# Spreading the RMS-norm factors of an encoder trunk: four fp32 matmuls on a diagonal, or two wide ones on its rounded parts

## The chip, the cores and the metric

One core of a Trainium2 chip runs the whole kernel in one launch. The metric is device microseconds of an execution, least is best. "Before" has three timed runs and one profiled execution.

## The reference

One layer on 2048 tokens of width 1024. Two sub-layers each begin with an RMS norm, scaled and shifted by a conditioning vector:

```python
def rmsnorm(x, g):
    y = x * lax.rsqrt(jnp.mean(x * x, axis=-1, keepdims=True) + EPS)
    return y * g
...
mod = silu(c) @ w_ada + b_ada
sh1, sc1, gt1, sh2, sc2, gt2 = split(mod, 6)
h = rmsnorm(x, g_norm1) * (1.0 + sc1) + sh1
proj = h @ w_in                                  # q, k, v of two groups of 8 heads
o_sb = stick_breaking_attention(...)             # strictly causal
o_ca = chunked_relpos_attention(...)             # own chunk of 64 and 8 before, learned bias
x = x + gt1 * (concat(o_sb, o_ca) @ w_o)
h = rmsnorm(x, g_norm2) * (1.0 + sc2) + sh2
x = x + gt2 * (square(relu(h @ w1)) @ w2)
```

All data is float32. What the change touches is the row of factors rsqrt(mean(x*x) + EPS), one factor for each token.

## The kernel before

Activations lie transposed: features on the 128 partitions, tokens along the free axis, in four blocks of 512 tokens (tb 0 to 3). A tile of 128x512 is one of eight feature slices of a block. Nearly every large product is done three times on rounded parts: an operand is split into a high part, rounded to the type that TensorE takes at one matmul a product (F32R in the code), and a low part, the rest; high x high, high x low and low x high add up in PSUM.

There are three stages. The first projects: block 3 comes first, with its weights, then the blocks 2, 1 and 0 are normed while the projections of the block before go on. The attention stage runs units of one head and one block of queries; between its steps it places further projections and parts of the output projection. The MLP runs its two products as seven products of half-size blocks each (classes First and Second), with the norms of blocks 1 and 0 put between the first steps of a Second phase.

A norm has these steps. ScalarE squares the eight slices and VectorE adds them up (norm_sums; norm2 for the MLP). TensorE sums over the partitions with four matmuls that use the sums as the stationary operand and a column of ones (norm_columns): this leaves the tokens on the partitions, 128 x 4 numbers. VectorE scales them and GpSimd takes the power and one refining step (norm_powers, rsqrt). To bring the factors back to one row that every partition holds, VectorE multiplies the identity with them (norm_diagonal: four diagonal blocks of 128x128 side by side), and TensorE multiplies a 128x128 matrix of ones with the diagonals (norm_spread: four fp32 matmuls of 128 columns). VectorE then multiplies x by the result in PSUM (first stage, tile names pra) or copies it into a row tile (MLP, psr).

Seven norms are spread this way. The first one, block 3 of the first stage, has its own code and calls norm_spread itself. Three go through start_norm (L464) for the blocks 2, 1 and 0 of the first stage. Two in the attention stage (tile prm) are written out in finish_row. Two go through norm2 (L1329) in the MLP. start_norm and norm2 call norm_rstd (L194) in a job called second, and the spread in a job called third some steps later; the jobs stand in lists that count steps.

The order of work is the program's: TensorE is kept in the order of the code, so are ScalarE, VectorE and GpSimd in the first stage, and nearly every DMA is issued on SyncE's queue.

Memory is given out in pools, those of the left side upward and those marked right downward. Left in the first stage stand, in this order: cpool (constants), rp, ring, hxp, np_ (the norms' tiles, L252), padn (a tile of 128 bytes that nothing uses, L253), stp (staging, tag st of six buffers of 128x2x512, L255) and wp (nine weight parts, L256). The staging ring takes every tile that is stored to DRAM. In the MLP, right: accp (tag c, twelve buffers of 128x512, function kept), hop 0 and 1 (split activations h) and np2; hop 2 and 3 are on the left.

In the attention stage each finished pair of heads is split into a tile os, of which there is one buffer, and stored to scr_m (function keep, L734).

Of the kernel before, what the change touches and what calls it, by code (L numbers as in the profile page):

```python
# [9 lines left out]
F32 = mybir.dt.float32  # L10
F32R = mybir.dt.float32r
BF16 = mybir.dt.bfloat16
AF = mybir.ActivationFunctionType
ALU = mybir.AluOpType
# [4 lines left out]
P = 128  # L19
# [6 lines left out]
TB = 512  # L26
# [53 lines left out]
def encoder_kernel(ctx, tc, xT, c, g1, g2, w_in, w_rest, gqk, bias, w_o, w1, w2, w_ada, b_ada, out):  # L80
    nc = tc.nc
    act, dve, pool, sp = nc.scalar, nc.vector, nc.gpsimd, nc.sync
    pe = Ordered(tc, nc.tensor)
# [3 lines left out]
    cpool = ctx.enter_context(tc.tile_pool(name="cpool", bufs=1))  # L87
# [27 lines left out]
    ident = cpool.tile([P, P], F32, name="ident")  # L115
    make_identity(nc, ident)
    ones = cpool.tile([P, P], F32, name="ones")
    pool.memset(ones, 1.0)
    zero = cpool.tile([P, 1], F32, name="zero")
    pool.memset(zero, 0.0)  # L120
    mhalf = cpool.tile([P, 2 * NH], F32, name="mhalf")
# [29 lines left out]
    def norm_sums(pl, src, tg, eng=None, square=None):  # L151

        acc = pl.tile([P, TB], F32, tag="nsa", name=f"nsa{tg}")
        for k in range(KT):
            x = src(k)
            if k == 0:
                act.activation(acc, x, AF.Square)
                continue
            sq = square(k) if square else pl.tile([P, TB], F32, tag="nsq", name=f"nsq{tg}_{k}")
            if square and k == KT - 1:  # L160
                pool.tensor_tensor(sq, x, x, op=ALU.mult)
                sq, last = last, sq
            else:
                act.activation(sq, x, AF.Square)
            if square and k == KT - 2:
                last = sq
                continue
            (eng or dve).tensor_tensor(acc, acc, last if square and k == KT - 1 else sq, op=ALU.add)
        if square:
            dve.tensor_tensor(acc, acc, sq, op=ALU.add)  # L170
        return acc

    def norm_columns(pp, acc, tg):
        pv = pp.tile([P, TB], F32, tag="ps", name=f"pv{tg}")
        for i in range(4):
            pe.matmul(pv[:, i : i + 1], acc[:, i * P : (i + 1) * P], ones[:, 0:1], start=True, stop=True)
        return pv

    def norm_powers(pl, pv, tg):
        v = pl.tile([P, 4], F32, tag="nv", name=f"nv{tg}")  # L180
        dve.tensor_scalar(v, pv[:, 0:4], 1.0 / D, EPS, op0=ALU.mult, op1=ALU.add)
        y = pl.tile([P, 4], F32, tag="ny", name=f"ny{tg}")
        t = pl.tile([P, 4], F32, tag="nt", name=f"nt{tg}")
        rsqrt(y, v, t)
        return y

    def norm_diagonal(pl, y, tg):
        dg = pl.tile([P, 4, P], F32, tag="ndg", name=f"ndg{tg}", bufs=1)
        dve.tensor_tensor(
            dg, ident.unsqueeze(1).to_broadcast([P, 4, P]), y.unsqueeze(2).to_broadcast([P, 4, P]), op=ALU.mult  # L190
        )
        return dg

    def norm_rstd(pl, pp, acc, tg, meanwhile=None):  # L194
        y = norm_powers(pl, norm_columns(pp, acc, tg), tg)
        if meanwhile:
            meanwhile()
        return norm_diagonal(pl, y, tg)

    def norm_spread(pp, dg, tg):  # L200
        pr = pp.tile([P, TB], F32, tag="ps", name=f"pr{tg}")
        for i in range(4):
            pe.matmul(pr[:, i * P : (i + 1) * P], ones, dg[:, i, :], start=True, stop=True)
        return pr
# [42 lines left out]
    pa, er = ctx.enter_context(ExitStack()), ctx.enter_context(ExitStack())  # L247
    if True:
# [1 line left out]
        adaw = er.enter_context(tc.tile_pool(name="adaw", bufs=4, side="right"))  # L250
        hp = er.enter_context(tc.tile_pool(name="hp", bufs=1, side="right"))
        np_ = pa.enter_context(tc.tile_pool(name="np_", bufs=2))  # L252
        padn = pa.enter_context(tc.tile_pool(name="padn", bufs=1))  # L253
        padn.tile([P, 32], F32, tag="pad", name="padn")
        stp = pa.enter_context(tc.tile_pool(name="stp", bufs=6))  # L255
        wp = pa.enter_context(tc.tile_pool(name="wp", bufs=WT))  # L256
        ppc = er.enter_context(tc.tile_pool(name="ppC", bufs=1, space=PSUM))
        pp, pq = Banks(zb), Banks(db)
# [80 lines left out]
        def stage(nm):  # L339
            return stp.tile([P, 2, TB], F32R, tag="st", name=f"st{nm}")  # L340
# [123 lines left out]
        def start_norm(tb, wait, more):  # L464
            tg = f"a{tb}"
            acc = norm_sums(np_, lambda k: xts[tb][k], tg)

            def second():
                dg = norm_rstd(np_, pq, acc, tg)

                def third():
                    r = norm_spread(pq, dg, tg)
                    for k, x in enumerate(xts[tb]):
                        dve.scalar_tensor_tensor(x, x, aff[:, 0, k : k + 1], r, op0=ALU.mult, op1=ALU.mult)

                norms.add(more, third)

            norms.add(wait, second)
# [18 lines left out]
        act, dve, pool = (Ordered(tc, e) for e in (act, dve, pool))  # L497
# [20 lines left out]
        for k in range(2):  # L518
            load_first(k)
        acc = norm_sums(  # L520
            np_, lambda k: xts[3][k], "a3",
            square=lambda k: stp.tile([P, TB], F32, tag="qh", name=f"nsqa3_{k}", bufs=6),
        )
# [15 lines left out]
        dg = np_.tile([P, 4, P], F32, tag="ndg", name="ndga3", bufs=1)  # L539
# [139 lines left out]
    if True:  # L679
# [536 lines left out]
        op = ph.enter_context(tc.tile_pool(name="op", bufs=2))  # L1216
# [14 lines left out]
        for i in range(len(steps) + LAG):  # L1231
# [29 lines left out]
            if i + 1 < len(steps):  # L1261
                u, st = steps[i + 1]
# [23 lines left out]
    if True:  # L1286
# [3 lines left out]
        accp = pm.enter_context(tc.tile_pool(name="accp", bufs=12, side="right"))  # L1290
        hop = {k: pm.enter_context(tc.tile_pool(name=f"hop{k}", bufs=1, side="right")) for k in range(2)}
        np2 = pm.enter_context(tc.tile_pool(name="np2", bufs=2, side="right"))
        pp = Banks(zb, zb, ab, db, zb, zb, ab, db)
# [18 lines left out]
        def temp(nm):  # L1312
            return tp.tile([P, TB], F32, tag="t", name=f"t{nm}")
# [4 lines left out]
        def bank(nm):  # L1318
            return pp.tile([P, TB], F32, tag="ps", name=f"ps{nm}")
# [3 lines left out]
        def at(n, job):  # L1323
            jobs.setdefault(n, []).append(job)
# [4 lines left out]
        def norm2(tb, step):  # L1329

            acc = rp.tile([P, TB], F32, tag="r", name=f"r{tb}")
            xs = {}

            def load(k):
                xs[k] = temp(f"xn{tb}_{k}")
                sp.dma_start(xs[k], scr_x[tb, k])

            def add(k):
                x = xs.pop(k)
                act.activation(x if k else acc, x, AF.Square)  # L1340
                if k:
                    dve.tensor_tensor(acc, acc, x, op=ALU.add)

            def second():
                dg = norm_rstd(np2, pp, acc, f"m{tb}")

                def third():
                    pr = bank(f"r{tb}")
                    for i in range(4):
                        pe.matmul(pr[:, i * P : (i + 1) * P], ones, dg[:, i, :], start=True, stop=True)  # L1350
                    dve.tensor_copy(acc, pr)
                    rows[tb] = acc

                later.add(2, third)

            for k in range(KT):
                at(step + k, lambda k=k: load(k))
                at(step + k + 4, lambda k=k: add(k))
            at(step + KT + 4, lambda: later.add(2, second))

        def right_blocks(mb, k, home):
# [307 lines left out]
        for mb in (1, 0):  # L1669
            begin = len(steps)  # L1670
            steps += [First(mb, j, i) for j in range(NP) for i in PRODUCTS]
            for j in range(NP):
                f = steps[begin + 7 * j]
# [122 lines left out]
```

## Time and profile before

| | |
|---|---|
| median of three runs | 2605.78 us (2605.65, 2605.78, 2612.86) |
| profiled execution, its own time | 2608.17 us |
| its span, first to last instruction | 2606.5 us |
| TensorE busy | 2563.8 us, 98% |
| VectorE busy | 1889.6 us, 72% |
| ScalarE busy | 1406.3 us, 54% |
| GpSimd busy | 945.5 us, 36% |
| bytes moved by DMA | 640.18 MB, mean 246 GB/s |

The profile names lines as L42 for nearly every instruction, since one helper there records them; so rows are told apart by tiles, written out<-in with buffer numbers left out. PE is TensorE, PEld its weight loads, DVE VectorE, ACT ScalarE, POOL GpSimd, SPq the DMA queue of SyncE. A row of the timeline has start, duration, engine, line, operation, tiles, shape and count, and in brackets how long the engine had been idle and what ended it. A row of a waits view has the waiting tile, the one that released it, the total in us, the times and the longest. A row of a view by stretches has the stretch, its length, the busy time of PE, PEld, DVE, ACT and POOL, the granted TensorE clock, the DMA share and GB/s. The first stage lasts to about 430 us, the attention stage to about 1310, the MLP to the end.

### The profile page before, as it was taken

The page shows a single profiled execution, that of the slowest core. Times are in us where ns is not written, and L with a number is a line of the kernel's source. Part 1 is how long each engine was busy: PE and PEld are TensorE (multiplying, and loading weights), DVE is VectorE, ACT ScalarE, POOL GpSimd, SP SyncE. Part 2 cuts the span into 40 slices and gives each one's busy share as a digit, 9 for nine tenths or more (in the row PEclk, how much of TensorE's full clock was granted, in tenths as well). Part 3 has the DMA queues.
Part 4 walks back from the last instruction along what each step waited for, and adds up shares of the span by engine and source line. Part 5 has one row for each costly group of instructions (what it writes and reads, how often), then busy time and mean ns, then how long its engine had stood idle before and what let it go on. Part 6 is the DMA issues. An engine that isn't in the chain of part 4 may idle for free.

```text
span 2606.5 us, 39188 instructions
## 1 busy us (share of the span) xinstructions
PE 2563.8 (98%) x12528; PEld 2132.6 (82%) x12528; DVE 1889.6 (72%) x3235; ACT 1406.3 (54%) x2716; POOL 945.5 (36%) x1257
## 2 busy tenths in 40 slices
PE   7999999999999999999999999999999999999999
PEld 5888888788888888887888888888888888888887
DVE  7656767887689879998768787768766666555555
ACT  5333435668766676666744444556544444544443
POOL 4330144776666667676604333000002323200000
PEclk9999999999999999999999999999999999999999
DMA  9879979788876788756797777876764444375574
GB/s 341 323 299 362 338 286 284 217 252 271 274 242 214 239 273 272 235 193 201 218 345 248 250 260 271 298 277 229 256 220 175 149 150 154 125 263 198 197 270 154
DMA packets 251502, 640.18 MB, mean 246 GB/s; under 512 B 28576, under 2 KB 52128, under 8 KB 242208
## 3 DMA queue, kind: packets, MB, share of 16 engines
q1 hardware_dynamic: 250000, 632.96, 71.0%
q10 hardware_dynamic: 1296, 4.72, 0.4%
q8 instruction: 99, 1.62, 0.3%
q14 instruction: 107, 0.88, 0.1%
HBM read 446.20 MB, written 191.37 MB: 245 GB/s over the span
## 4 chain that ended last, share of the span: by engine, by line
PE 84%; DVE 6%; ACT 3%; DMA 3%; issue 2%; POOL 1%; SPq 0%; DVEq 0%; POOLq 0%; ACTq 0%
PE ps L42 41%; PE pt L42 11%; PE acc L42 6%; PE wt L42 6%; PE pf L42 4%; PE z L42 4%; PE po L42 4%; PE pq L42 3%; PE cz L42 2%; DVE p L42 1%; PE pso L42 1%; PE ct L42 1%; DMA scr_m<-os 1%; ACT z L42 1%; DVE w2s L42 1%
## 5 line engine op out<-in xcount | busy, mean ns | idle before, releaser
L42 PE MATMUL ps<-oph,opv 128*128 128x512 f32 x2688 | 611.8, 389 | 0.1
L42 PE MATMUL ps<-h,opw 128*128 128x512 f32 x2664 | 605.2, 389 | 0.0
L42 PEld LDWEIGHTS ps<-oph,opv 128*128 128x128 f32 x2688 | 503.9, 188 | 106.2 <-DVE opv L42 0.8
L42 PEld LDWEIGHTS ps<-h,opw 128*128 128x128 f32 x2664 | 499.5, 188 | 105.4 <-DVE cx L42 1.2
L42 POOL TENSOR_TENSOR b<-p 128x512 f32<-128x512 f32 (+1 forms) x320 | 292.0, 912 | 171.0 <-DVE p L42 88.2
L42 ACT CAST wth<-wt 128x512 fp32r<-128x512 f32 (+3 forms) x544 | 256.9, 483 | 169.7 <-PE wt L42 160.2
L42 DVE TENSOR_TENSOR wtl<-wt,wth 128x512 fp32r<-128x512 f32 (+3 forms) x544 | 290.7, 546 | 67.5 <-ACT wth L42 65.2
L42 DVE TENSOR_TENSOR oph<-hw,oph 128x512 fp32r<-128x512 f32 x224 | 156.1, 697 | 215.0 <-ACT oph L42 214.9
L42 ACT CAST oph<-hw 128x512 fp32r<-128x512 f32 x224 | 139.3, 622 | 277.3 <-PE ps L42 268.0
L42 PE MATMUL pt<-w,ht 128*128 128x512 f32 x1248 | 288.2, 391 | 0.0
L42 POOL TENSOR_TENSOR ts<-w 128x512 f32<-128x512 f32 x32 | 47.9, 1496 | 660.7 <-DMA w<-in_w_dram 618.3
L42 PEld LDWEIGHTS pt<-w,ht 128*128 128x128 f32 x1248 | 232.9, 188 | 47.7
L42 DVE TENSOR_TENSOR_SCAN p<-z,p,zero 128x512 f32<-128x512 f32 x192 | 245.5, 1280 | 24.1 <-ACT z L42 17.6
L42 PE MATMUL acc<-wth,v 128*128 128x512 f32 (+3 forms) x544 | 221.0, 410 | 0.0
L42 ACT ACTIVATE z<-z 128x512 f32<-128x512 f32 (+1 forms) x320 | 166.5, 521 | 56.6 <-PE z L42 50.7
L42 PE MATMUL z<-k,q 128*128 128x512 f32 (+3 forms) x640 | 186.1, 372 | 8.2 <-DVE p L42 7.5
L42 PE MATMUL acc<-wtl,v 128*128 128x512 f32 (+3 forms) x544 | 185.8, 348 | 0.0
L42 DVE TENSOR_TENSOR opw<-w,opw 128x512 fp32r<-128x512 f32 x127 | 101.1, 798 | 113.5 <-ACT opw L42 113.3
L42 POOL TENSOR_TENSOR e<-e,cols 128x640 f32<-128x640 f32 (+4 forms) x128 | 142.7, 1120 | 83.9 <-DVE cols L42 55.2
L42 PE MATMUL wt<-ident,b 128*128 128x128 f32 x1088 | 171.4, 273 | 1.1 <-DVE cols L42 0.5
L42 PEld LDWEIGHTS wt<-ident,b 128*128 128x128 f32 x1088 | 136.3, 140 | 42.2 <-DVE cols L42 1.9
L42 PE MATMUL po<-fx,ow 128*128 128x512 f32 x576 | 161.6, 393 | 0.0
(196 smaller groups left out, 4097.1 us busy)
## 6 DMA issues: line engine op xcount, KB each, us to landing
hw<-scr_hid SPq DMA_DIRECT2D x112, 512.0 KB, 4.1
q<-scr_q SPq DMA_DIRECT2D x128, 256.0 KB, 5.1
w<-in_w_dram SPq DMA_DIRECT2D x64, 512.0 KB, 5.2
hw<-scr_s SPq DMA_DIRECT2D x64, 512.0 KB, 4.7
k<-scr_k SPq DMA_DIRECT2D x240, 128.0 KB, 4.6
v<-scr_v SPq DMA_DIRECT2D x120, 256.0 KB, 4.3
wa<-in_w_ada_dram SPq DMA_DIRECT2D x48, 512.0 KB, 6.6
ow<-scr_wo SPq DMA_DIRECT2D x24, 1024.0 KB, 6.0
```

What stands on the lines that cost most here:

```text
L42: return lambda *x, **y: self.tc.keep_in_program_order(f(*x, **y))
```

## The change

The three norms of start_norm and the two of norm2 get another spread. norm_rstd rounds the factors to a high part yh and takes the rest yl; VectorE multiplies the identity with each, which gives two diagonal tiles of 128x512 in the rounded type. norm_row then multiplies a rounded matrix of ones with each of the two in one matmul of 512 columns, and they add up in PSUM. In the first stage the two diagonals share one buffer of the staging ring; in the MLP they take two buffers of accp. GpSimd makes the rounded ones once, at the start. np_ gets two small tags and the pad padn is dropped; in np2 the old diagonal's tag falls away. The order of all other instructions on every engine, and of all DMAs, stays the same.

```diff
+    ones_r = cpool.tile([P, P], F32R, name="ones_r")
+    pool.tensor_copy(ones_r, ones)
...
-    def norm_rstd(pl, pp, acc, tg, meanwhile=None):
+    def norm_rstd(pl, pp, acc, tg, dg):
+
         y = norm_powers(pl, norm_columns(pp, acc, tg), tg)
-        if meanwhile:
-            meanwhile()
-        return norm_diagonal(pl, y, tg)
+        yh = pl.tile([P, 4], F32R, tag="nyh", name=f"nyh{tg}")
+        yl = pl.tile([P, 4], F32, tag="nyl", name=f"nyl{tg}")
+        dve.tensor_copy(yh, y)
+        dve.tensor_tensor(yl, y, yh.bitcast(F32), op=ALU.subtract)
+        for l, part in enumerate((yh.bitcast(F32), yl)):
+            dve.tensor_tensor(
+                dg[l].rearrange("p (i f) -> p i f", f=P), ident.unsqueeze(1).to_broadcast([P, 4, P]),
+                part.unsqueeze(2).to_broadcast([P, 4, P]), op=ALU.mult,
+            )
+        return dg
+
+    def norm_row(pr, dg):
+
+        for l in range(2):
+            pe.matmul(pr, ones_r, dg[l], start=l == 0, stop=l == 1)
+        return pr
...
-        padn = pa.enter_context(tc.tile_pool(name="padn", bufs=1))
-        padn.tile([P, 32], F32, tag="pad", name="padn")
...
             def second():
-                dg = norm_rstd(np_, pq, acc, tg)
+                st = stage(f"ndg{tg}")
+                dg = norm_rstd(np_, pq, acc, tg, [st[:, l, :] for l in range(2)])
 
                 def third():
-                    r = norm_spread(pq, dg, tg)
+                    r = norm_row(pq.tile([P, TB], F32, tag="ps", name=f"pr{tg}"), dg)
...
             def second():
-                dg = norm_rstd(np2, pp, acc, f"m{tb}")
+                dg = norm_rstd(np2, pp, acc, f"m{tb}", [
+                    accp.tile([P, TB], F32R, tag="c", name=f"ndgm{tb}_{l}") for l in range(2)
+                ])
 
                 def third():
-                    pr = bank(f"r{tb}")
-                    for i in range(4):
-                        pe.matmul(pr[:, i * P : (i + 1) * P], ones, dg[:, i, :], start=True, stop=True)
+                    pr = norm_row(bank(f"r{tb}"), dg)
                     dve.tensor_copy(acc, pr)
```

## The prediction, made before the changed kernel was run

> **What bounds the kernel now.** I read the page's shares first, then the waits of TensorE, then the stages, then the timeline around each place that the change touches.
>
> ```profile
> PE 2563.8 (98%) x12528; PEld 2132.6 (82%) x12528; DVE 1889.6 (72%) x3235; ACT 1406.3 (54%) x2716; POOL 945.5 (36%) x1257
> ...
> PE 84%; DVE 6%; ACT 3%; DMA 3%; issue 2%; POOL 1%; SPq 0%; DVEq 0%; POOLq 0%; ACTq 0%
> ...
> PE pva L42 <- DVE nsaa L42: 13.6, 1, 13.6
> PE z L42 <- DVE p L42: 7.5, 16, 1.2
> PE wt L42 <- DVE wtl L42: 3.7, 1, 3.7
> ...
> PE psr L42 <- DVE ndgm L42: 0.8, 1, 0.8
> ```
>
> TensorE is busy 98% of the span and carries 84% of the chain that ended last. It is idle for 2606.5 - 2563.8 = 42.7 us in all, and a third of that is one wait of 13.6 us at the start for the first norm, whose spread this change leaves as it is. So an edit moves the time in two ways only: by the TensorE time that it adds or removes, and by making TensorE wait where it does not wait now. Of the waits above one belongs to the edited code: psr waits 0.8 us for ndgm.
>
> **What is replaced on TensorE.** Five norms are edited: three in the first stage (tile pra) and two in the MLP (psr). In the list by time the columns are start, duration, engine, line, operation, tiles, shape and count.
>
> ```profile
> 81.19 1.06 PE L42 MATMUL pra<-ndga,ones 128*128 128x128 f32 x8
> 82.01 18.20 PE L42 MATMUL pt<-w,ht 128*128 128x512 f32 x79
> ...
> 253.85 1.05 PE L42 MATMUL pra<-ndga,ones 128*128 128x128 f32 x8
> 254.67 7.54 PE L42 MATMUL pt<-w,ht 128*128 128x512 f32 x32
> ...
> 310.15 1.06 PE L42 MATMUL pra<-ndga,ones 128*128 128x128 f32 x8
> 310.97 9.36 PE L42 MATMUL pt<-w,ht 128*128 128x512 f32 x40
> ...
> 1705.57 1.16 PE L42 MATMUL psr<-ndgm,ones 128*128 128x128 f32 x8 [0.80 <-DVE ndgm L42]
> 1706.48 16.59 PE L42 MATMUL ps<-oph,opv 128*128 128x512 f32 x72
> ...
> 1729.31 1.06 PE L42 MATMUL psr<-ndgm,ones 128*128 128x128 f32 x8
> 1730.12 5.05 PE L42 MATMUL ps<-oph,opv 128*128 128x512 f32 x21
> ```
>
> A matmul's own duration overlaps its neighbours', so I price by starts. From the start of the four old matmuls (eight records, two to each) to the start of what follows pass 0.82, 0.82, 0.82, 0.91 and 0.81 us. The new form is two matmuls of 512 columns on rounded operands, the kind of the neighbouring rows: 16.59 us for 72 of them is 0.230 us each, so 0.46 us a norm. Where TensorE does not wait, a norm gains 0.82 - 0.46 = 0.36 us.
>
> Beside this stands a rule of the Trainium skill, page "FP8 and Floating Point Precision", section "TensorE Precision Notes": true fp32 takes four passes through the array, and the reduced form reads the fp32 and truncates it. If the reduced form takes one pass, the old spread streams 4 x 4 x 128 = 2048 columns and the new one 1024, which would halve 0.82 to 0.41 and raise the gain of a norm by 0.05, the sum by about 0.2 us; the row of 0.230 us for a matmul of the new kind decides.
>
> **What is added on VectorE.** In place of one product of the identity with the factors there are four instructions: a copy of 128x4 that rounds, a subtraction of 128x4 for the rest, and two products of 128x512. The places, one for each stage, and the nearest small operation (cv, 128x8):
>
> ```profile
> 74.26 0.69 DVE L42 TENSOR_TENSOR ndga<-ident,nya 128x512 f32<-128x512 f32 x1 [2.25 <-POOL nya L42]
> ...
> 76.58 0.69 DVE L42 TENSOR_REDUCE cv<-csq 128x8 f32<-128x512 f32 x1 [1.62 <-ACT csq L42]
> 77.30 0.17 DVE L42 TENSOR_SCALAR cv<-cv 128x8 f32<-128x8 f32 x1
> ...
> 242.04 0.69 DVE L42 TENSOR_TENSOR ndga<-ident,nya 128x512 f32<-128x512 f32 x1 [2.31 <-POOL nya L42]
> ...
> 306.97 0.69 DVE L42 TENSOR_TENSOR ndga<-ident,nya 128x512 f32<-128x512 f32 x1 [2.31 <-POOL nya L42]
> ...
> 1704.82 0.69 DVE L42 TENSOR_TENSOR ndgm<-ident,nym 128x512 f32<-128x512 f32 x1 [2.25 <-POOL nym L42]
> 1705.43 0.68 DVE L42 TENSOR_TENSOR oph<-hw,oph 128x512 fp32r<-128x512 f32 x1
> 1706.03 0.69 DVE L42 TENSOR_TENSOR opv<-hw,opv 128x512 fp32r<-128x512 f32 x1
> ...
> 1726.30 0.69 DVE L42 TENSOR_TENSOR ndgm<-ident,nym 128x512 f32<-128x512 f32 x1 [2.24 <-POOL nym L42]
> ```
>
> The two small ones at 0.17 us each are 0.34; then the first product; the second starts 0.60 later, as opv does behind oph (1705.43 to 1706.03), and lasts 0.69. The second part is therefore ready 0.34 + 0.60 + 0.69 = 1.63 us after the factors, where the one diagonal was ready after 0.69: 0.94 us later. A product into the rounded type is no dearer: oph's is 0.68.
>
> Who waits for this? In the first stage the parts are ready at 74.26 + 1.63 = 75.89, at 243.67 and at 308.60; TensorE comes for them at 81.19, 253.85 and 310.15. It waits at none, with 5.3, 10.2 and 1.5 us to spare. Behind the products on VectorE is queued the work on cv (76.58, after 1.62 us of idleness) or a pass of sv or cv that slips by at most 0.94 us into idle time like it. That cover costs nothing; gone, it would cost up to 0.94 us a norm. In the MLP the second of the two is ready at 1726.30 + 1.63 = 1727.93 against 1729.31: no wait either.
>
> The first of the two is the one that already waits. The second part comes at 1704.82 + 1.63 = 1706.45; TensorE starts about 0.06 us after it, as now (1705.51 to 1705.57), and has done the first matmul by then; the second takes 0.23, and ps goes on at 1706.74 instead of 1706.48: 0.26 us lost. Queued behind on VectorE are oph and opv, 0.94 us later, for a later step: TensorE's next 72 matmuls stand without a wait now.
>
> **Edits that I cost at nothing.** One copy of 128x128 on GpSimd for the rounded ones, ahead of the memset of zero:
>
> ```profile
> 1.17 0.29 POOL masks.py:199 TENSOR_SCALAR_AFFINE_SELECT ident<-ident 128x128 f32<-128x128 f32 x1
> ...
> 2.08 0.20 ACT L42 ACTIVATE cg<-zero 128x1 f32<-128x1 f32 x1
> 3.97 0.63 ACT L42 ACTIVATE nsaa<-xt 128x512 f32<-128x512 f32 x1 [1.69 <-DMA xt<-in_xT_dram]
> ```
>
> Nearest row 0.29 us. ScalarE's first activation needs zero at 2.08 and then waits 1.69 us for a DMA, which hides it; uncovered it is 0.3 us.
>
> In the first stage the parts lie in a buffer of the staging ring (stp, tag st, six buffers), so the first product must also wait until the store that last used its buffer has landed.
>
> ```profile
> L42 SPq DMA_DIRECT2D scr_q<-stf x4: 319/326/336, 58.0 to 60.0; - x4
> ...
> DMA to landing us min/median/max: 7.6/9.0/10.5
> ```
>
> For the first norm these are such stores: the last is issued at 60.0 and lands by 70.5, before 74.26 by 3.8 us. The other two buffers were last stored at about 222 and 289, 18 us and more before their products. The ring then runs one buffer further for three stores, and its users keep at least five.
>
> Dropping the pad: the two new tags of 4 values add to the pool in front what the pad gave up, so the large tiles behind it keep their place to each other; the rounded ones push all pools on the left side up by 512 bytes against those on the right. Does a place cost anything?
>
> ```profile
> L42 PE MATMUL ps<-h,opw x2664: 387/389/501, 1381.7 to 2297.0; 128*128 128x512 f32 x191
> ...
> L42 PE MATMUL po<-fx,ow 128*128 128x512 f32 x576 | 161.6, 393 | 0.0
> ```
>
> The tiles h lie half in pools that move and half in pools that stay (hop 0 and 1 right, 2 and 3 left), and the least and the median over all 2664 are 387 and 389 ns. I take 0. The upper bound is the 4 ns between these two rows, on 5352 such matmuls of the MLP: 21 us. I see no bound below that excludes a gain, but no row shows one.
>
> **The sum.** 4 x (-0.36) + 0.26 = -1.2 us. Against the profiled execution, 2608.17 us (span 2606.5 and 1.67 around it), that is 2607.0. The median of the three runs, 2605.78, is 2.4 us lower than that execution; I apply the change to it: **2604.6 us**. With the cover of VectorE everywhere the end is 5 x (-0.36) = -1.8; with none, 5 x (0.94 - 0.36) = +2.9: 2604.0 to 2608.7. A measurement of this kernel can hardly tell less than 0.3%, 7.8 us, from no change, so even this whole span counts as no change.
>
> **The rivals.** What is larger than the edit is a stall in the attention stage, where ScalarE waits for the store that frees the only buffer os:
>
> ```profile
> 707.50 0.62 ACT L42 CAST os<-o 128x512 fp32r<-128x512 f32 x1 [4.54 <-DMA scr_m<-os]
> ...
> 708.99 1.94 PE L42 MATMUL wt<-ident,e 128*128 128x128 f32 x8 [3.72 <-DVE wtl L42]
> ...
> 700.00:720.00 20.00, 16.28 (x84) 14.12 (x83) 10.32 (x28) 12.43 (x30) 11.25 (x16) 0.83 0.76 237
> ...
>   DMA scr_m<-os: 7.6, 3
> ...
> DMA to landing us min/median/max: 2.6/3.0/8.1
> ```
>
> One store of 32 took 8.1 us instead of 3.0. TensorE stood for 3.72 us, and its granted clock over these 20 us was 0.83: 20 x 0.17 = 3.4 us more. Together 7.1 us. The Trainium skill, page "TensorE: Matmul & The Clock Gate", section "Part 1: The HAM clock gate", says that an idle window of about 3.4 us brings the clock to half until TensorE has been busy for another; by that rule the trace agrees, 3.72 us and then 0.83.
>
> - Faster: the edit shifts the stage by a microsecond and this store no longer meets the loads. 2605.78 - 7.1 - 1.2 = **2597.5 us**. For it: one wait of 4.54 us among 32 stores is chance. Against it: nothing in the edit touches these queues, and the timed runs may not have had the stall. Chance 0.14.
> - Slower: the same mechanism strikes at two more turns of the attention stage. It decides where a store of os lands so late that TensorE stands for more than some 3.5 us. 2604.6 + 2 x 7.1 = **2618.8 us**. For it: three waits of this kind exist, 7.6 us in all; the slowest of the three timed runs, 2612.86, lies 7.1 us above the median, just one such stall. Chance 0.10. One more stall alone gives 2604.6 + 7.1 = 2611.7, still no change by the bound: 0.08.
> - Layout: the shift of 512 bytes does cost TensorE up to 4 ns a matmul: up to 2604.6 + 21 = 2626 us, and over the bound from 11 us of it on. Only h speaks, and against it. Chance 0.08.
> - The change does not do what it says, and the copies and waits eat the gain: up to 2608.7, inside the forecast's own span, so no case of its own.
>
> **How the numbers follow.** The forecast has 0.60. No change: 0.60 + 0.08 = 0.68. Faster 0.14. Slower 0.10 + 0.08 = 0.18. The range takes in 2597.5 below and 2611.7 with the jitter of a run above, 2597 to 2613; outside lie the two slower cases, 0.18.
>
> **What would show it.** Right: pra and psr with two matmuls a norm and 0.46 us to the next start; four new VectorE rows of 0.17, 0.17, 0.69 and 0.69; at the first psr a wait for ndgm of about 1.1 us before the first matmul and of 0.4 before the second, and none at the other four places; mean matmul durations of 389 ns unchanged. Wrong: a wait of ndga for a store (the ring), a mean of 391 or more in the MLP (the layout), or another number of stretches with a clock below 0.9 between 430 and 1310 us (the stall). A time outside 2598 to 2613 is not the norms.

## The result and the profile after

The changed kernel takes 2616.73 us (median of 14 runs, 2611.70 to 2622.20), the kernel before it 2608.30 us beside it (14 runs, 2605.05 to 2613.06). The ratio is 1.0028, 95% interval 1.0018 to 1.0037: slower by 8 us, about the 0.3% that the prediction took as the least that can be told, and outside its range. Two more comparisons, below, gave 1.0040 and 1.0035. Its profiled execution has a span of 2616.7 us and a time of 2618.44.

The page after, first part: TensorE's busy time is what it was (2563.8), while the span is 10.2 us longer.

```profile
PE 2564.1 (98%) x12498; PEld 2130.0 (81%) x12498; DVE 1893.0 (72%) x3250; ACT 1406.9 (54%) x2716; POOL 940.2 (36%) x1258
```

The list of TensorE by time, after (start, duration, engine, line, operation, tiles, shape, count, idle time before and its releaser):

```profile
79.81 0.64 PE L42 MATMUL pra<-stndga,ones_r 128*128 128x512 f32 x2
80.29 9.96 PE L42 MATMUL pt<-w,ht 128*128 128x512 f32 x43
...
252.12 0.63 PE L42 MATMUL pra<-stndga,ones_r 128*128 128x512 f32 x2
253.74 0.50 PE L42 MATMUL pt<-w,ht 128*128 128x512 f32 x1 [0.98 <-ACT w L42]
254.46 7.78 PE L42 MATMUL pt<-w,ht 128*128 128x512 f32 x33 [0.23 <-DVE w L42]
...
299.10 1.05 PE L42 MATMUL pva<-ones,nsaa 128*128 128x1 f32 x8 [1.05 <-DVE nsaa L42]
300.36 0.51 PE L42 MATMUL pt<-w,ht 128*128 128x512 f32 x1 [0.20 <-ACT w L42]
301.08 10.96 PE L42 MATMUL pt<-w,ht 128*128 128x512 f32 x47 [0.22 <-DVE w L42]
...
1716.30 1.11 PE L42 MATMUL psr<-ndgm,ones_r 128*128 128x512 f32 x2 [0.99 <-DVE ndgm L42]
1717.24 16.54 PE L42 MATMUL ps<-oph,opv 128*128 128x512 f32 x72
...
1740.02 0.64 PE L42 MATMUL psr<-ndgm,ones_r 128*128 128x512 f32 x2
1740.50 9.73 PE L42 MATMUL ps<-oph,opv 128*128 128x512 f32 x42
```

The spread itself does as forecast: 0.48 us from its first start to what follows. But behind the second of these norms, block 1's, stand two waits for weights, and at 299 us three more: one for the sums of block 0's norm (nsaa) and two for weights. Before has no wait at either place: its row of 254.67 is shown above, and this is the other:

```profile
299.12 11.19 PE L42 MATMUL pt<-w,ht 128*128 128x512 f32 x48
```

Who was late? ScalarE by time, the changed kernel first, then the kernel before:

```profile
246.92 0.37 ACT L42 CAST sv<-pt 128x256 fp32r<-128x256 f32 x1 [3.30 <-PE pt L42]
252.79 0.37 ACT L42 CAST sv<-pt 128x256 fp32r<-128x256 f32 x1 [5.50 <-PE pra L42]
253.06 4.26 ACT L42 CAST w<-wr 128x512 fp32r<-128x512 f32 x8
```

```profile
248.65 0.37 ACT L42 CAST sv<-pt 128x256 fp32r<-128x256 f32 x1 [3.30 <-issue]
249.51 0.37 ACT L42 CAST sv<-pt 128x256 fp32r<-128x256 f32 x1 [0.49 <-DVE sv L42]
249.78 4.27 ACT L42 CAST w<-wr 128x512 fp32r<-128x512 f32 x8
```

The second cast of sv waits 5.50 us for pra, a matmul that has nothing to do with it but the memory: block 1's two diagonals lie in a buffer of the staging ring, made here on VectorE and read only at 252.12.

```profile
240.32 0.17 DVE L42 CAST nyha<-nya 128x4 fp32r<-128x4 f32 x1 [2.31 <-POOL nya L42]
240.52 0.16 DVE L42 TENSOR_TENSOR nyla<-nya,nyha 128x4 f32<-128x4 f32 x1
240.60 0.68 DVE L42 TENSOR_TENSOR stndga<-ident,nyha 128x512 fp32r<-128x512 f32 x1
241.21 0.69 DVE L42 TENSOR_TENSOR stndga<-ident,nyla 128x512 fp32r<-128x512 f32 x1
```

In the order of the program the next tiles of the ring are woh, wol and two of sv. The first three do not wait for pra, so they took other buffers; the second sv does, so it was handed the diagonals' own. (The trace does not name buffers; this is read from the waits.) ScalarE works in the order of the program, so the eight weight casts behind that sv start at 253.06 instead of 249.78, and TensorE waits for them. SyncE issues in that order too: the store of this sv goes out at 258.99 instead of 255.70, and block 0's eight loads behind it at 284.32 instead of 280.67. The rows are those of SyncE and of ScalarE's first work on xt, the changed kernel first:

```profile
258.99 1.24 SPq L42 DMA_DIRECT2D scr_v<-sv  x2
...
284.32 7.71 SPq L42 DMA_DIRECT2D xt<-in_xT_dram  x8
...
292.27 0.63 ACT L42 ACTIVATE nsaa<-xt 128x512 f32<-128x512 f32 x1 [3.82 <-DMA xt<-in_xT_dram]
```

```profile
255.70 1.24 SPq L42 DMA_DIRECT2D scr_v<-sv  x2
...
280.67 8.31 SPq L42 DMA_DIRECT2D xt<-in_xT_dram  x8
...
289.22 0.63 ACT L42 ACTIVATE nsaa<-xt 128x512 f32<-128x512 f32 x1 [0.35 <-DMA xt<-in_xT_dram]
```

The buffers of these loads were not what was late: the products on VectorE that free them (ht<-xt) begin at 279.14 us after the change and at 279.56 before it. Nor was ScalarE, which stands idle for 3.82 us until the first load lands.

The same matmuls can be paired between two traces, in their order. The shift of their starts against before goes from -1.73 us at 240 to -0.42 at 256 and +1.32 at 425: the first stage loses 3.05 us from this point on. Behind it the shift grows to +10.2 at the end, by 4.4 at 640 to 700 (a stall of os; before has its own at 704, which gives 1.7 back) and by 4.8 at 1374 to 1384 (the start of the MLP).

### The profile page after: what moved, and what is told of

The parts are those of the page before. It is cut to its first block, busy times and chain, and to the rows that moved or that the text cites. A ratio compares the mean times of both kernels' runs of the same rounds, so it can differ in the third digit from the quotient of the medians.

```text
span 2616.7 us, 39131 instructions
## 1 busy us (share of the span) xinstructions
PE 2564.1 (98%) x12498; PEld 2130.0 (81%) x12498; DVE 1893.0 (72%) x3250; ACT 1406.9 (54%) x2716; POOL 940.2 (36%) x1258
```

## The experiments

Theory: the loss comes from the buffer of the ring that block 1's diagonals hold. Rivals: the new spread in the MLP, the shift of the layout, the ring being one buffer short at all three norms, chance. One run, x_on_gpsimd, is not in the table and stands by itself below.

All are compared with the kernel before on the same chip. The table stands ahead of the single experiments. "Swing" is how much later the same matmuls start at 425 us than they did at 240 us, against before; "behind" is the same from 425 us to the end. Both are of one profile each.

| run | median, before beside it | ratio, 95% interval | sv waits for pra | swing | behind |
|---|---|---|---|---|---|
| the change | 2616.73, 2608.30 | 1.0028, 1.0018 to 1.0037 | 5.5 | +3.05 | +8.9 |
| after_again | 2615.33, 2607.50 | 1.0040, 1.0027 to 1.0052 | 5.5 | +4.00 | +1.6 |
| after_third | 2617.78, 2607.44 | 1.0035, 1.0022 to 1.0047 | 5.5 | +5.31 | +5.9 |
| first_only | 2615.75, 2607.50 | 1.0033, 1.0021 to 1.0045 | 5.5 | +6.40 | +3.4 |
| ring_only | 2612.53, 2608.16 | 1.0018, 1.0009 to 1.0026 | 5.9 | +4.70 | +4.3 |
| ring_again | 2613.56, 2607.44 | 1.0025, 1.0016 to 1.0034 | 5.9 | +3.54 | -1.9 |
| own_buffer | 2606.03, 2608.16 | 0.9993, 0.9982 to 1.0005 | none | -0.87 | -0.5 |
| block1_own | 2610.52, 2607.50 | 1.0011, 1.0000 to 1.0023 | none | -0.85 | +5.6 |
| early_spread | 2607.38, 2607.50 | 1.0005, 0.9991 to 1.0019 | none | -0.32 | -4.0 |
| late_spread | 2610.84, 2608.29 | 1.0007, 0.9998 to 1.0017 | none | -0.82 | +2.8 |
| mlp_only | 2607.74, 2608.16 | 0.9997, 0.9988 to 1.0006 | none | 0.00 | -4.3 |
| layout_only | 2608.01, 2608.16 | 0.9997, 0.9987 to 1.0008 | none | 0.00 | +3.1 |

**own_buffer: the whole change, the first stage's diagonals in a buffer of their own.**

```diff
-                st = stage(f"ndg{tg}")
+                st = np_.tile([P, 2, TB], F32R, tag="ndg", name=f"ndg{tg}", bufs=1)
```

(One buffer of nsa is given up for the room, and the first norm's old diagonal shares the tag.)

> The whole change, but the diagonals of the three first-stage norms lie in a buffer of their own (4 KB under the old diagonal's tag; the sums' tag nsa gets one buffer instead of two to make room) and not in the staging ring; the large pools lie where the changed kernel has them. Ring theory (a diagonal holds a staging buffer until its spread, ScalarE waits for that, and the later loads slip): no wait of sv for pra, no wait of pt for w near 254 us, the attention stage begins 1 to 2 us earlier than before instead of 1.4 us later, and the time is within 2 us of before or 1 us under it. Layout theory (the 512 bytes cost): slower than before by 5 to 8 us all the same. MLP theory (the two spreads there do it): slower by 5 to 8 us, with the loss after 1370 us.

The loss is gone. ScalarE by time in own_buffer:

```profile
249.00 0.37 ACT L42 CAST sv<-pt 128x256 fp32r<-128x256 f32 x1 [0.49 <-DVE sv L42]
249.27 4.27 ACT L42 CAST w<-wr 128x512 fp32r<-128x512 f32 x8
```

Two norms lie between 240 and 425 us, and the shift falls by 0.87 us there: 0.43 a norm, where the prediction had 0.36.

**ring_only: the old spread, with its one fp32 diagonal in the ring; nothing else.**

```diff
-                dg = norm_rstd(np_, pq, acc, tg)
+                st = stage(f"ndg{tg}")
+                y = norm_powers(np_, norm_columns(pq, acc, tg), tg)
+                dg = st[:, 0, :].bitcast(F32).rearrange("p (i f) -> p i f", f=P)
+                dve.tensor_tensor(dg, ident..., y..., op=ALU.mult)
```

> Before, with the old fp32 diagonal of the three first-stage norms put into a buffer of the staging ring; no rounded parts, no wide products, old layout, pad kept. Ring theory: ScalarE's sv waits some 5.5 us for pra near 247 us, pt waits for w, the first stage ends about 3 us later than before, and the time is 3 to 8 us above before. Layout and MLP theories: as before, within 1 us.

The ring alone, with none of the new products or matmuls, costs 4.4 us. The waits view of its first stage has the same rows as the change:

```profile
ACT sv L42 <- PE pra L42: 5.9, 1, 5.9
PE pt L42 <- ACT w L42: 1.2, 2, 1.0
```

**mlp_only and layout_only: the two other parts.** The first keeps the old spread, pad and diagonals in the first stage; the second is the kernel before with an unused rounded ones, which pushes the left side up by 512 bytes.

```diff
 # mlp_only, against the change
-                st = stage(f"ndg{tg}")
-                dg = norm_rstd(np_, pq, acc, tg, [st[:, l, :] for l in range(2)])
+                dg = norm_old(np_, pq, acc, tg)
...
-                    r = norm_row(pq.tile([P, TB], F32, tag="ps", name=f"pr{tg}"), dg)
+                    r = norm_spread(pq, dg, tg)
 # layout_only, against before
+    ones_r = cpool.tile([P, P], F32R, name="ones_r")
+    pool.tensor_copy(ones_r, ones)
```

> Only the two norms of the MLP get the new spread; the three of the first stage keep the old one and the old diagonal, the rounded ones and the pad are there. Ring theory: within 1 us of before, the first stage as before. Layout theory: slower by 5 to 8 us. MLP theory: slower by 4 to 8 us with the loss after 1370 us.

> Before, with the rounded ones made and used by nobody: all pools of the left side lie 512 bytes higher, nothing else changes. Ring and MLP theories: as before, within 1 us. Layout theory: slower by 5 to 8 us.

Both take the time of before to 0.1%, and by the intervals (up to 1.0006 and 1.0008) neither can have cost more than about 2 us. Neither part has a measurable share in the loss.

**first_only, and the change twice more (after_again, after_third) with ring_again.** first_only has the change in the first stage and the old spread in the MLP:

```diff
-                dg = norm_rstd(np2, pp, acc, f"m{tb}", [
-                    accp.tile([P, TB], F32R, tag="c", name=f"ndgm{tb}_{l}") for l in range(2)
-                ])
+                dg = norm_old(np2, pp, acc, f"m{tb}")
...
-                    pr = norm_row(bank(f"r{tb}"), dg)
+                    pr = bank(f"r{tb}")
+                    for i in range(4):
+                        pe.matmul(pr[:, i * P : (i + 1) * P], ones, dg[:, i, :], start=True, stop=True)
```

> The first stage's three norms as in the change, ring buffers and pad included; the two norms of the MLP as in before. Ring theory: the whole loss is in the first stage, so the wait of sv for pra (5.5 us) is there and the time is 4 to 8 us above before, within 2 us of the changed kernel. Rival (the MLP's spread brings part of the loss by what it does to VectorE at its start): the loss is 4 us, that of the ring alone, and the changed kernel beside it is 3 us slower still.

> The changed kernel once more, beside the kernel before, to see which of its losses come back. Ring theory (the buffer of block 1's diagonals is handed to a weight cast of the same block): the wait of sv for pra of about 5.5 us and a swing of TensorE's starts of +3 to +4 us between 240 and 302 us come back, and the time is 4 to 8 us above before. If the rest of the loss belongs to the edit, the late start of the MLP (+4.8 us between 1374 and 1384 us) and the stall of os at 640 us come back too, and the time is 7 to 8 us above; if these were chance, their places change and the swing at 302 us alone stays.

The first stage alone has the loss of the whole. The late start of the MLP that the first profile showed (+4.8 us from 1374 to 1384) was +0.7 in after_again and -0.2 in after_third, so that place does not belong to the edit: it changes from one execution to the next.

> The changed kernel beside the ring alone, on the same chip. If the ring is the whole loss: both 4 to 9 us above before and within 2 us of each other, the swing of TensorE's starts from 240 to 425 us +3 to +6 us in both, and what comes behind 425 us differs in sign and place from profile to profile. If the new spread brings a loss of its own: this kernel is 3 us or more slower than the ring alone, with no overlap of the intervals.

> The old spread, its one diagonal in the staging ring, nothing else changed. If the ring is the whole loss: 4 to 9 us above before, within 2 us of the changed kernel beside it, wait of sv for pra 5.9 us. If the new spread brings a loss of its own: 3 to 5 us above before, 3 us or more below the changed kernel.

Side by side the change and the ring alone are 10.3 and 6.1 us above before, and their intervals overlap (1.0022 to 1.0047, 1.0016 to 1.0034). Neither wording came true: the ring is the larger part of the loss, and the 4.2 us between the two are not settled.

**block1_own: only block 1's diagonals outside the ring.**

```diff
-                st = stage(f"ndg{tg}")
+                st = np_.tile([P, 2, TB], F32R, tag="ndg", name=f"ndg{tg}", bufs=1) if tb == 1 else stage(f"ndg{tg}")
```

(Room is made as in own_buffer.)

> The full change, but block 1's two diagonals lie in a buffer of their own; those of blocks 2 and 0 stay in the staging ring. Ring theory in its narrow form (only block 1's buffer is held across casts that need it): no wait of sv for pra, and a time within 2 us of before. If the ring costs at every one of the three places, running one buffer short: 2 to 4 us above before.

The wait is gone and the swing is -0.85 as in own_buffer. Block 0's norm lies in that stretch too, and from 60 to 240 us, where block 2's lies, the shift falls by 0.41. So blocks 2 and 0 take the ring for nothing, and only block 1 pays. The time is 3.0 us above before, more than the 2 I had allowed: this profile's loss lies behind 425 us, 3.0 of it between 1500 and 1700, where the ring is not in use by a norm.

**early_spread and late_spread: the place where the spread is written.** Both keep everything in the ring and move block 1's spread in the program by two steps forward or one back.

```diff
-                start_norm(1, 5, 3)
+                start_norm(1, 5, 1)      # early_spread
+                start_norm(1, 5, 4)      # late_spread
```

> The full change in the staging ring, but block 1's spread comes two steps earlier, so that its buffer is free before the cast of sv that gets it. Ring theory: pra at about 245 to 249 us instead of 252, the wait of sv below 1 us, and a time within 2 us of before. If the loss comes from the ring's place in memory or from its queue being one buffer shorter, not from how long the buffer is held: 4 us or more above before as with the ring alone.

> The full change in the staging ring, but block 1's spread comes one step later, so the buffer is held some 5 us longer. Theory of the handing-out: buffers are given in the order in which the program is written; with the spread written behind the cast of sv, the ring cannot give that cast the held buffer and passes on to the next one. So no wait of sv for pra, TensorE's starts between 240 and 425 us move by less than 1 us, and the time is within 2 us of before. Rival (the holding itself costs: one buffer fewer for as long as it is held): a longer hold makes it worse, a wait of sv of 5 to 11 us, and 8 us or more above before.

These two tell the hold from the handing-out. The spread by time, early_spread first, then late_spread:

```profile
241.51 1.10 PE L42 MATMUL pra<-stndga,ones_r 128*128 128x512 f32 x2
```

```profile
257.84 0.64 PE L42 MATMUL pra<-stndga,ones_r 128*128 128x512 f32 x2
```

In early_spread pra comes at 241.51 (earlier than I expected: two steps are 10.6 us), and no sv waits for it. In late_spread the diagonals keep their buffer until 257.84, one step longer than in the change, and yet nobody waits. That fits what was expected: sv is written ahead of the spread there, so the ring cannot hand it a buffer still in use by a later line. Which buffer it gave instead the trace does not show. ScalarE by time in late_spread:

```profile
247.19 0.37 ACT L42 CAST sv<-pt 128x256 fp32r<-128x256 f32 x1 [3.29 <-PE pt L42]
248.06 0.37 ACT L42 CAST sv<-pt 128x256 fp32r<-128x256 f32 x1 [0.49 <-DVE sv L42]
248.33 4.27 ACT L42 CAST w<-wr 128x512 fp32r<-128x512 f32 x8
```

The time of late_spread is 2.6 us above before, more than the 2 expected; in its profile the shift from 425 us on is +2.8, and in the first stage it is -0.82.

So the length of the hold is not what costs. What costs, as these runs have it, is that the spread is written just ahead of sv: in the program the buffer counts as free by then, while on the chip it comes free only 5.5 us after sv could have used it.

**x_on_gpsimd: block 0's loads on another queue.** This was to separate the two parts of the loss, late weights and late loads.

```diff
-                load_x(0)
+                load_x(0, pool)
```

> The full change, but block 0's eight loads of xt are issued from GpSimd's queue instead of SyncE's. The loss in the first stage has two parts by the theory: the late weight casts (TensorE waits for w, 1.2 + 0.2 to 0.4 us) and the late xt loads behind the late stores on SyncE's in-order queue (the rest, 2 to 4 us between 297 and 302). Theory: the wait of sv for pra (5.5 us) and the waits for w stay, +1.3 us at 256 as in the change, and the second part at 297 to 302 goes; the time is 2 to 4 us less than that of the changed kernel, 3 to 6 us above before. Rival (the second part comes from ScalarE being late itself, not from the queue): the swing at 297 to 302 stays, and the time is that of the changed kernel, 7 to 9 us above before.

It takes 2631.80 us, ratio 1.0093 (1.0081 to 1.0106), and decides nothing: GpSimd sends the loads some 6 us apart at first and 3 to 4 us later on, the last at 307.95 us, and TensorE waits 12.69 us for the sums that need them. GpSimd, then TensorE by time:

```profile
281.75 0.55 POOL L42 DMA_DIRECT2D xt<-in_xT_dram  x1 [23.69 <-DVE ht L42]
288.34 0.55 POOL L42 DMA_DIRECT2D xt<-in_xT_dram  x1 [6.04 <-issue]
294.89 0.55 POOL L42 DMA_DIRECT2D xt<-in_xT_dram  x1 [6.00 <-issue]
...
312.21 1.87 PE L42 MATMUL pva<-ones,nsaa 128*128 128x1 f32 x8 [12.69 <-DVE nsaa L42]
```

That the loads are late because they stand behind the store on SyncE is thus read from the rows of 258.99 and 284.32 and from the idle ScalarE, and was not shown by an experiment.

**The size of the loss.** Two stretches of the first stage show what TensorE loses. The columns are stretch, length, busy PE, PEld, DVE, ACT, POOL, granted clock, DMA share, GB/s; the fences are the change, first_only, after_third and early_spread:

```profile
250.00:270.00 20.00, 18.80 (x82) 14.99 (x81) 15.27 (x27) 6.56 (x15) 0.29 (x2) 1.00 0.61 213
290.00:310.00 20.00, 18.53 (x84) 14.91 (x83) 12.54 (x22) 11.09 (x21) 1.80 (x5) 1.00 0.89 329
```

```profile
290.00:310.00 20.00, 18.08 (x70) 14.15 (x69) 12.80 (x21) 10.72 (x21) 0.00 (x0) 0.83 0.89 324
```

```profile
290.00:310.00 20.00, 17.90 (x74) 14.12 (x74) 12.54 (x22) 11.10 (x21) 1.27 (x3) 0.91 0.90 321
```

```profile
250.00:270.00 20.00, 20.00 (x90) 16.57 (x89) 10.83 (x21) 6.77 (x16) 0.29 (x2) 1.00 0.74 270
290.00:310.00 20.00, 20.00 (x93) 16.62 (x93) 15.96 (x31) 10.46 (x21) 2.84 (x6) 1.00 0.94 349
```

At 250 to 270 TensorE idles 1.2 us in each of the six profiles of the table that have the wait of sv, and never in the others. At 290 to 310 it idles 0.6 to 2.1 us, and in four of the six the granted clock drops as well: in first_only 1.92 us idle and 20 x 0.17 = 3.4 us of clock make 5.3, and the shift there grows by some 5.2. Without that part of the clock, 20 us x (1 - granted clock), the six swings are 3.05, 2.2, 3.5, 3.0, 2.9 and 3.5 us in the order of the table: much of their scatter is the clock.

The four profiles with the full first-stage edit and the hold swing by +4.69 us in the mean, the four of own_buffer, block1_own, early_spread and late_spread by -0.72: 5.4 us apart. In medians against before they lie +8.7 and +0.8 us: 7.9 apart. So some 5.4 of 7.9 us are in the first stage, in these rows. The remaining 2.5 us are less than single profiles scatter behind 425 us (-4.3 to +8.9), and whether they belong to the edit stays open.

No version here beats the kernel before by more than the interval: own_buffer has 0.9982 to 1.0005.

## Why the prediction was wrong

- **The failed step** is "The ring then runs one buffer further for three stores, and its users keep at least five", costed at nothing. It asked who had the buffer before the diagonals, and when that store landed; no ndga waited for a store, as it said. It did not ask who gets the buffer after them. That was an sv of the projection under way, which then waited 5.5 us for pra. Its list of signs named a wait of ndga for a store; the wait that came was that of a later user for ndga's reader. The count of buffers was right and beside the point, as late_spread and block1_own show. In size: 0 forecast, some 5 us in the first stage. (Of the 12.1 us between 2604.6 and 2616.73, 2.5 are the base: before takes 2608.30 here, and 2605.78 in the three runs that the forecast started from.)
- **The sign of what could be late.** I listed who waits for the edited work (TensorE for the diagonals: 10.2 us to spare at block 1) and took a large slack as safety. In a shared buffer that slack is also the time for which the buffer is held.
- **The spread.** 0.48 us from start to start against 0.46 forecast (252.12 can't be read, a wait lies behind it). Four VectorE rows of 0.17, 0.16, 0.68 and 0.69 us, as forecast. The 0.48 us are 0.24 us a matmul, nearer to the row's 0.230 than to half of the 0.41 us a norm that was estimated from the Trainium skill's four passes.
- **The first psr.** Forecast: a loss of 0.26 us. Wait 0.99 and 0.94 to the next start are 1.93 us, against 0.80 + 0.91 = 1.71 before: 0.22 us lost.
- **The layout.** Taken at 0, bound 21 us. layout_only is at 0.9997, and the MLP's matmuls have kept their time, by the tile view of h after:

```profile
L42 PE MATMUL ps<-h,opw x2664: 387/389/501, 1391.1 to 2307.2; 128*128 128x512 f32 x191
```

- **The rivals.** The slower one was the stall of os at more turns. After has one such stall at 640 us instead of the one at 704, the same number, and it did not decide the sign. That the time landed near 2618.8 is luck and no support for it. The sum of -1.2 us would have been the forecast without the ring: the four kernels without the hold are at 0.9993 to 1.0011, where 1.2 us can't be told from nothing.

## What to carry over

Before putting a tile into a shared ring, look at who is handed its buffer next: as these runs have it, the ring gives buffers out in the order of the program, so a tile that is written early and read late can block a later, unrelated writer, and with it what is written behind that writer on its engine and on SyncE. A slack of 10 us ahead of the reader is a hold of 10 us; it costs nothing (blocks 2 and 0, late_spread) unless the ring hands that buffer to a writer who is due before the read. Where the room for an own buffer is lacking, moving the last reader a step behind the next writer, so that the ring must pass on, took the wait away as moving it ahead did.

## What the hardware showed beyond that

The granted clock dropped after short idle times. The Trainium skill, page "TensorE: Matmul & The Clock Gate", section "Part 1: The HAM clock gate", asks for an idle window of about 3.4 us. Here after_third went to 0.91 with 1.68 + 0.20 + 0.22 us of idle time at 299 to 302 us, and first_only to 0.83 with 1.72 + 0.20. after_again with 0.77 + 0.20 and ring_only with 0.17 + 0.20 + 0.23 went to 0.91 as well, while the change with 1.05 + 0.20 + 0.22 and ring_again with 0.62 + 0.20 + 0.23 kept 1.00. Measured, the drop came well below that window and not every time, and the sum of the idle times does not tell when; what does stays open.

At the start of the MLP VectorE's two-input products took 1.56 to 1.78 us instead of 0.68 while GpSimd summed weights. VectorE, GpSimd and TensorE by time, after:

```profile
1373.76 0.68 DVE L42 TENSOR_TENSOR cy<-cy,cy 128x512 f32<-128x512 f32 x1
...
1375.03 1.56 DVE L42 TENSOR_TENSOR h<-cy,h 128x512 fp32r<-128x512 f32 x1
1376.51 1.78 DVE L42 TENSOR_TENSOR cy<-cy,cy 128x512 f32<-128x512 f32 x1
...
1374.75 1.29 POOL L42 TENSOR_TENSOR ts<-w 128x512 f32<-128x512 f32 x1 [56.71 <-DMA w<-in_w_dram]
1376.12 1.62 POOL L42 TENSOR_TENSOR ts<-ts,w 128x512 f32<-128x512 f32 x1
...
1382.89 0.73 PE L42 MATMUL ps<-h,opr 128*128 128x512 f32 x2 [2.67 <-ACT opr L42]
```

The Trainium skill, page "SBUF — State Buffer", section "Who interferes with whom", says that a VectorE instruction with two inputs in SBUF contends with a GpSimd instruction that reads SBUF; by that the trace agrees, 1.78 us against 0.68. No experiment here took the overlap away.
